# Tree attention on one core: three stores one block of loads back, and three heads instead of two stored apart in pieces of 116 rows

## The chip, the cores and the metric

The kernel runs on one core of a Trainium2 chip. The core has five instruction streams that run beside each other and meet at semaphores: TensorE (PE in the profile, with its weight loads as PEld), VectorE (DVE), ScalarE (ACT), GpSimd (POOL) and SyncE (SP). Data moves between HBM and the on-chip memory SBUF through 16 DMA engines, which POOL, SP and ACT feed with transfers. The metric is the time of one execution on the device in microseconds (us), as the median of several runs. The profile is of one further execution.

## The reference

Q, K and V are float32 arrays of shape 8 x 12 x 512 x 64 (batch, heads, positions, dimension), which makes 96 independent heads. Position i is a node of a binary tree whose parent is (i - 1) // 2. A position attends to itself and to its ancestors only:

```python
scores = np.einsum('bhqd,bhkd->bhqk', Q, K) * scale          # scale = 1 / sqrt(64)
scores = scores + (1 - mask) * (-1e9)                        # mask: itself and its ancestors
weights = np.exp(scores - np.max(scores, axis=-1, keepdims=True))
weights = weights / (np.sum(weights, axis=-1, keepdims=True) + 1e-10)
return np.einsum('bhqk,bhkd->bhqd', weights, V).astype(np.float32)
```

Each of Q, K, V and the output has 12.58 MB, and one head of one array has 128 KB.

## The kernel before

The 96 heads are worked on in 48 pairs. The main loop runs over i, and in its round i it forms the scores of pair i on PE (`scores1`, `scores2`), takes their exponentials on ACT, multiplies the weights of pair i - 1 by V on PE (`values`) and divides by the sums on DVE (`norm`, the line L735, which writes the output tile `of`). Only those parts of the score matrix are formed that the tree can reach. In between, `turn` transposes K and Q of later pairs on PE (into `ktp` and `qtp`), and DVE copies the result to SBUF. DVE, ACT and POOL also lay out V in the form that `values` wants (`spread`, L374).

A head's 512 positions lie in SBUF as 128 partitions of 4 positions each, so that a partition of one head holds 1 KB of float32 output. In what follows a row is such a partition's 1 KB. Output tiles hold 8 heads (1 MB, heads 8b to 8b + 7 for block b), and from pair 16 on four consecutive pairs fill one tile: pair 36 has the heads 72 and 76, pair 37 has 73 and 77, pair 38 has 74 and 78, pair 39 has 75 and 79.

POOL issues nearly all DMAs. Loads of K and Q bring 8 heads at a time late in the kernel (`load_k`, `load_q` with the block's first head, 1 MB read from HBM and 512 KB written to SBUF, since the load turns float32 to bfloat16). Loads of V bring 16 heads in pieces (`load_rows`: `upper` is half of them, `leaves0` and `leaves1` a quarter each). A store of a block is 1 MB. All of POOL's transfers go through one queue (q0 in the profile, called software_dynamic). SP and ACT have queues of their own (q1 and q10, hardware_dynamic); they carry the first loads, the heads that are stored apart, and the last pairs' stores.

The order on POOL is a list, written by `pool_program` (L759). In each round, `pool(i)` (L878) takes operations from its front for as long as `ready` allows them; the operation is put into POOL's program there, and on the chip it then waits for its semaphores alone. Two kinds of waits matter. POOL's DMAs take turns on eight semaphores (DMASW0 to DMASW7), so that each waits until the eighth DMA before it has landed. And a load waits until the readers of its buffer are done (4 buffers each for K and Q, 3 for V, 10 output tiles).

In the list before, the loads of K and Q go from block 56 to block 88 in steps of 8 heads, and behind each pair of loads stands one store, 56 heads behind (`BEHIND`). `lay_beside` (L443) is a POOL copy of a whole K or Q tile into another layout, made for the blocks 80 and 88; the transposes of these blocks (L507, L566) read the copy. Behind the loads the list has the other stores, with the copies between them.

`store_apart` (L753) is called once, behind round 38. It stores the heads 72 and 73 from SP, each as 116 rows and as 12 rows. POOL's store of that block then has six heads instead of eight.

Of the kernel before, what the change touches and what calls it, by code (L numbers as in the profile page):

```python
# [10 lines left out]
CODE = 2048.0  # L11
CODE_ROWS = 40
NOUT = 20
BEHIND = 56

# [104 lines left out]
def kernel(  # L120
# [7 lines left out]
    nc = tc.nc  # L128
    B, H, S, D = Q.shape
    P = nc.NUM_PARTITIONS  # L130
    assert S == 512 and D == 64 and P == 128 and (B * H) % 4 == 0
    scale = float(1.0 / np.sqrt(D))
    NH = B * H
# [3 lines left out]
    KB, VB = 8, 16  # L137
# [459 lines left out]
    def scores1(i):  # L597

        sp = psS.tile([P, 2, 512], fp32, name="s1")
        for a in range(2):  # L600
            nc.tensor.matmul(  # L601
                out=sp[:, a, :],
                lhsT=(k1code if i < WIDE else k1wide)[64 * a:64 * a + CODE_ROWS, :],
                rhs=(q1code, q1wide, q1far)[(i >= WIDE) + (i >= FAR)][64 * a:64 * a + CODE_ROWS],
                start=True, stop=False,
            )
        for a in range(2):
            nc.tensor.matmul(  # L608
                out=sp[:, a, :], lhsT=keys(i, a, TOP),
                rhs=qTs[i][64 * a:64 * a + 64, :, :].rearrange("p t c -> p (t c)"),  # L610
                start=False, stop=True,
            )
        et = etpool.tile([P, 2, 4, 128], bf16, name="e1")
        nc.scalar.activation(  # L614
            out=et[:, :, :, :].rearrange("p a t c -> p (a t c)"),
            in_=sp[:, :, :].rearrange("p a c -> p (a c)"),
            func=AF.Exp, scale=scale,
        ) if i < WIDE else nc.scalar.activation(  # L618
            out=et[:, :, :, :].rearrange("p a t (r u) -> p a (t r) u", u=2 if i < FAR else 4),
            in_=sp[:, :, :].rearrange("p a (u c) -> p a c u", u=2 if i < FAR else 4),  # L620
            func=AF.Exp, scale=scale,
        )
        ets[i] = et
# [102 lines left out]
    def norm(i):  # L726
        j, r = divmod(i, 4)
        if r == 0:
            ofs[j] = opool.tile([P, 8, 4, D], fp32, name="of")
        o4 = obs[i][:, :, 0:260].rearrange("p a (t c) -> p a t c", c=D + 1)  # L730
        rec = small.tile([P, 2, 4, 1], fp32, name="rec")
        for a, n in ((0, 2),) if i < NP - 1 else ((0, 1), (1, 1)):
            nc.vector.reciprocal(out=rec[:, a:a + n, :, :], in_=o4[:, a:a + n, :, D:D + 1])  # L733
            h0, h1 = [head(i, x) % 8 for x in (a, a + n - 1)]
            nc.vector.tensor_tensor(  # L735
                out=ofs[j][:, h0:h1 + 1:head(i, 1) - head(i, 0), :, :],
                in0=o4[:, a:a + n, :, 0:D],
                in1=rec[:, a:a + n, :, :].to_broadcast([P, n, 4, D]),
                op=ALU.mult,
            )  # L740

    def store(eng, h0, n, step=1, p0=0, p1=P):
        return eng.dma_start(  # L743
            out=Or[p0:p1, h0:h0 + step * (n - 1) + 1:step, :],
            in_=ofs[h0 // 8][p0:p1, h0 % 8:h0 % 8 + step * (n - 1) + 1:step, :, :].rearrange(
                "p h t d -> p h (t d)"
            ),
        )


    APART, APART_AT, APART_ROWS = 72, 38, 116

    def store_apart():  # L753

        for p0, p1 in ((0, APART_ROWS), (APART_ROWS, P)):
            for h in range(2):
                store(nc.sync, APART + h, 1, 1, p0, p1)

    def pool_program():  # L759

        ops = [
            (load_k, 2, 2), (load_q, 2, 2), (load_v, 0, 4), (load_v, 4, 4),
            (load_k, 4, 2), (load_k, 6, 2), (load_q, 4, 2), (load_k, 8, 4),
            (load_q, 6, 2), (load_q, 8, 4), (load_v, 8, 8), (load_k, 12, 4),
            (load_q, 12, 4), (load_k, 16, 4), (load_rows, 1, "upper"),
            (load_q, 16, 4), (load_rows, 1, "even"), (load_k, 20, 4), (load_rows, 1, "odd"),
            (load_q, 20, 4), (load_k, 24, 8), (load_q, 24, 4), (load_rows, 2, "upper"),
            (load_q, 28, 4), (load_rows, 2, "leaves0", "leaves1"), (load_k, 32, 8), (load_q, 32, 8),
            (load_rows, 3, "upper"),
            (spread_pool, (1, "Z0", 8, 16), (1, "Z1", 8, 16), (1, 6, 8, 16), (1, 9, 8, 16)),  # L770
            (load_q, 40, 8), (load_k, 40, 8), (load_rows, 3, "leaves0", "leaves1"), (load_k, 48, 8),
            (spread_top, 2), (spread_pool, (2, "Z0", 0, 16), (2, "Z1", 0, 16)), (load_q, 48, 8),
            (spread_pool, (2, "X", 0, 16), (2, "M", 0, 16), (2, "D1", 0, 16)), (spread_top, 3, 0, 12),
            (load_rows, 4, "upper"), (spread_top, 3, 12, 16),
        ]
        loaded, stored = 72, 0
        for h in range(56, NH, KB):
            top = [(spread_top, h // VB + 0)] if h % VB == 8 and 4 <= h // VB + 0 < NH // VB else []
            if top:
                top.append((spread_pool, (h // VB, "Z0", 0, 16), (h // VB, "Z1", 0, 16)))  # L780
            ops += [(load_k, h, KB)] + top + [(load_q, h, KB)]
            if h == 64:
                ops.append((
                    spread_pool, *[(3, part, 0, 16) for part in ("Z0", "Z1", "X", "M", "D1")]
                ))
            while loaded < min(h + 32, NH):
                names = ("leaves0", "leaves1") if loaded % VB else ("upper",)
                ops.append((load_rows, loaded // VB) + names)
                loaded += KB
            if top:  # L790
                o = h // VB
                ops.append((spread_pool, *[(o, part, 0, 16) for part in ("X", "M", "D1")]))
            if stored + KB + BEHIND <= h + KB:
                ops.append((store, nc.gpsimd, stored, KB))
                stored += KB
        ops.insert(-1, (lay_beside, "kst", 80 // KB))
        while stored < NH - KB:
            n = 2 if stored == APART else 0
            ops.append((store, nc.gpsimd, stored + n, KB - n))
            if stored == 40:  # L800
                ops.append((lay_beside, "qst", 80 // KB))
            if stored == 64:
                ops += [(lay_beside, "kst", 88 // KB), (lay_beside, "qst", 88 // KB)]
            stored += KB
        ops += [(store, nc.gpsimd, NH - KB + h, 2) for h in (0, 4)]
        return ops

# [57 lines left out]
    def spread_by(copy, table, steady, i):  # L865
# [7 lines left out]
        for args in todo:  # L873
            spread(copy, *args)

    program = pool_program()

    def pool(i):  # L878
        while program and ready(program[0], i):
            op = program.pop(0)  # L880
            op[0](*op[1:])
# [18 lines left out]
    for i in range(NP + 1):  # L900
        steps = FIRST[i] if i < len(FIRST) else "SVK" if i % 2 else "SVQ"
        if i >= max(FAR, KFAR - 4):
            steps = ("SVK", "SVQ", "SVK", "SQV")[i % 4]
        elif i == FAR - 1:
            steps = "SQVK"
        for step in steps:
            if step == "S" and i < NP:
                scores1(i)
                scores2(i)
            if step == "V" and i >= 1:  # L910
                values(i - 1)
# [12 lines left out]
            if step == "D":  # L924
                spread_by(nc.vector.tensor_copy, BY_VECTOR, STEADY_VECTOR, i)
            if step == "A":
                spread_by(nc.scalar.copy, BY_SCALAR, STEADY_SCALAR, i)
        if "D" not in steps:
            spread_by(nc.vector.tensor_copy, BY_VECTOR, STEADY_VECTOR, i)
        if "A" not in steps:  # L930
            spread_by(nc.scalar.copy, BY_SCALAR, STEADY_SCALAR, i)
        pool(i)
        if i == APART_AT:
            store_apart()
        if i == NP - 1:
            for p in (0, P // 2):
                for a, eng in enumerate((nc.sync, nc.scalar)):
                    store(eng, head(i - 1, a), 1, 1, p, p + P // 2)
# [34 lines left out]
```

## Time and profile before

| | us |
|---|---|
| median of 3 runs (lowest, highest) | 132.93 (132.81, 133.04) |
| the profiled execution, its own time | 132.49 |
| its span, from the first instruction to the last | 130.7 |
| PE busy in it | 113.7 (87%) |
| DVE busy | 105.6 (81%) |
| ACT busy | 101.1 (77%) |
| POOL busy | 84.4 (65%) |
| granted TensorE clock, mean | 0.986 |

The profiled execution is 0.44 us under the median, and 1.8 us of its time lie outside the span. The first load of K lands near 4.5 us, the last work on DVE ends at 127.0 us, and what then follows up to the span's end is the landing of the last stores.

How to read the rows that follow. A row of a timeline gives the start in us from the span's start, the duration, the engine, the line, the operation and its tiles (out<-in), and in brackets the idle time before it and what ended it. For SP and ACT queues the row covers several issues from the first to the last. A row of the windows gives a stretch, its length, the busy time of each engine with its number of instructions, the TensorE clock, the mean busy share of the 16 DMA engines and the rate in GB/s of what was written. Packets of a DMA engine can overlap, so that the share of busy DMA engines can lie above 1. A row of a DMA queue gives the number of packets, the MB written and the time of the packets as a share of 16 engines' time in that stretch. MB are millions of bytes, KB are 1024.

### The profile page before, as it was taken

To read this page: it belongs to the slowest core of one execution; us is meant where nothing else is said; L and a number is where in the kernel's file an instruction comes from. 1 tells how busy PE (TensorE), PEld (TensorE's weight loads), DVE (VectorE), ACT (ScalarE), POOL (GpSimd) and SP (SyncE) were. 2 spreads that over 40 slices of the span, in tenths; PEclk is the share of its full clock that TensorE was granted. 3 is DMA by queue.
4 is the path that set the end of the run, shared out by engine and by line. 5 is a ranking of instruction groups with operands and counts; after the bars stand their busy time and mean duration, and the time that the engine had idled before them with its cause. 6 is when DMAs were issued, how large, how long until landed. Compare 5 with 4: busy or idle time off the path is not lost.

```text
span 130.7 us, 5436 instructions
## 1 busy us (share of the span) xinstructions
PE 113.7 (87%) x2353; PEld 81.0 (62%) x2353; DVE 105.6 (81%) x254; ACT 101.1 (77%) x163; POOL 84.4 (65%) x116
## 2 busy tenths in 40 slices
PE   6688969999799887899998999896999997999940
PEld 2354755766577566677776786674677675776630
DVE  3349779888999998989998998987898997894560
ACT  4179676989779995968987799797689785889930
POOL 6999625354483999995299899953999963202130
PEclk9999999999999999999999999999999999999995
DMA  2999999999999999999999999999999999999984
GB/s 89 248 190 192 201 195 201 201 202 205 201 203 208 208 205 207 208 210 205 207 211 201 283 292 210 270 309 231 338 228 322 257 277 397 402 404 386 382 339 145
DMA packets 26071, 32.25 MB, mean 247 GB/s; under 512 B 1240, under 2 KB 19544, under 8 KB 26048
## 3 DMA queue, kind: packets, MB, share of 16 engines
q0 software_dynamic: 24384, 30.41, 111.4%
q1 hardware_dynamic: 944, 0.91, 2.2%
q10 hardware_dynamic: 720, 0.59, 1.5%
q8 instruction: 18, 0.29, 0.8%
q14 instruction: 5, 0.04, 0.1%
HBM read 37.94 MB, written 12.58 MB: 386 GB/s over the span
## 4 chain that ended last, share of the span: by engine, by line
DVE 29%; DMA 28%; PE 22%; POOL 7%; ACT 6%; issue 4%; ACTq 0%; DVEq 0%; POOLq 0%
DMA vst<-in_V_dram 17%; DMA qst<-in_Q_dram 11%; DVE of L735 9%; PE ob L696 8%; DVE vt L374 6%; PE s L601 3%; DVE qq L577 3%; ACT e L652 3%; DVE rec L733 3%; DVE kk L521 3%; POOL kst L247 2%; PE s L608 2%; DVE kk L525 2%; POOL qst L247 2%; ACT e L618 2%
## 5 line engine op out<-in xcount | busy, mean ns | idle before, releaser
L618 ACT ACTIVATE e<-s 128x1024 bf16<-128x1024 f32 x40 | 40.9, 1024 | 15.0 <-PE s L608 14.6
L696 PE MATMUL ob<-vt,e 128*128 128x65 bf16 (+1 forms) x940 | 37.1, 197 | 2.6 <-DVE of L735 1.0
L696 PEld LDWEIGHTS <-e 128*128 128x128 bf16 (+1 forms) x960 | 30.1, 102 | 9.6 <-DVE of L735 1.9
L374 POOL COPY vt<-vst 32x512 int32<-32x512 int32 (+4 forms) x44 | 32.5, 739 | 4.7 <-PE ob L696 2.5
L652 ACT ACTIVATE e<-s 128x384 bf16<-128x384 f32 x80 | 34.7, 490 | 0.0
L735 DVE TENSOR_TENSOR of<-ob,rec 128x512 f32<-128x512 f32 x47 | 32.5, 691 | 1.6
L374 DVE COPY vt<-vst 32x1024 bf16<-32x1024 bf16 (+5 forms) x47 | 20.9, 445 | 2.8 <-DMA vst<-in_V_dram 1.9
L743 POOL DMA_DIRECT2D out_dram<-of x13 | 11.5, 888 | 12.9 <-DVE of L735 12.4
L733 DVE RECIPROCAL rec<-ob 128x8 f32<-128x8 f32 x47 | 9.5, 202 | 9.9 <-PE ob L696 9.3
L257 POOL DMA_DIRECT2D kst<-in_K_dram x11 | 8.0, 725 | 7.4 <-DMA qst<-in_Q_dram 3.2
L601 PE MATMUL s<-far,codes 40*128 40x512 bf16 x64 | 12.5, 386 | 0.0
L635 PEld LDWEIGHTS <-codes 40*128 40x128 bf16 x80 | 6.2, 94 | 8.7 <-issue 3.9
L614 ACT ACTIVATE e<-s 128x1024 bf16<-128x1024 f32 x8 | 8.2, 1023 | 4.1 <-PE s L608 4.0
L577 DVE COPY qq<-qtp 128x1024 bf16<-128x1024 bf16 x16 | 10.9, 680 | 0.3 <-PE qtp L572 0.3
L635 PE MATMUL s<-far,codes 40*128 40x384 bf16 x64 | 10.7, 324 | 0.4 <-ACT e L652 0.2
L257 POOL DMA_DIRECT2D qst<-in_Q_dram x12 | 8.5, 708 | 3.8 <-DMA vst<-in_V_dram 1.9
L374 ACT COPY vt<-vst 32x512 int32<-32x512 int32 (+3 forms) x19 | 10.4, 545 | 0.4
L608 PE MATMUL s<-qq,kk 64*128 64x512 bf16 x48 | 9.2, 378 | 1.0 <-DVE qq L577 1.0
L646 PEld LDWEIGHTS <-kk 64*128 64x128 bf16 x192 | 8.4, 94 | 2.6
L521 DVE COPY kk<-ktp 128x256 bf16<-128x256 bf16 x24 | 9.0, 414 | 0.7 <-PE ktp L513 0.7
L302 POOL DMA_DIRECT2D vst<-in_V_dram x7 | 5.6, 800 | 6.0 <-DMA vst<-in_V_dram 4.3
L572 PE MATMUL qtp<-ptile,qst 128*64 128x128 bf16 x192 | 7.5, 221 | 1.7 <-DVE qq L577 1.0
(64 smaller groups left out, 178.2 us busy)
## 6 DMA issues: line engine op xcount, KB each, us to landing
out_dram<-of POOLq DMA_DIRECT2D x10, 1024.0 KB, 15.2
kst<-in_K_dram POOLq DMA_DIRECT2D x9, 512.0 KB, 16.5
qst<-in_Q_dram POOLq DMA_DIRECT2D x8, 512.0 KB, 14.8
vst<-in_V_dram POOLq DMA_DIRECT2D x12, 256.0 KB, 13.5
vst<-in_V_dram POOLq DMA_DIRECT2D x6, 512.0 KB, 12.9
qst<-in_Q_dram POOLq DMA_DIRECT2D x6, 256.0 KB, 12.1
kst<-in_K_dram POOLq DMA_DIRECT2D x4, 256.0 KB, 10.3
out_dram<-of POOLq DMA_DIRECT2D x1, 768.0 KB, 13.0
```

The lines of the kernel that those rows point to most:

```text
L257: return nc.gpsimd.dma_start(out=kept[b][:, h0 % KB:h0 % KB + n, :, :].rearrange("p (g x) t d -> p g (x t d)", x=x), in_=src[:, h0 // x:(h ...
L374: return copy(out=dst, in_=src)
L521: nc.vector.tensor_copy(out=columns(flat, 32 * unit, (640, 4), (step, 2), (4, 8), (1, 4)), in_=columns(kp, base, (256, 4), (128, 2), (1, 8 ...
L577: nc.vector.tensor_copy(out=qqs[j][:, :, 8 * last:8 * last + 8, :].rearrange("p b u c -> p b (u c)"), in_=quarters,)
L601: nc.tensor.matmul(out=sp[:, a, :], lhsT=(k1code if i < WIDE else k1wide)[64 * a:64 * a + CODE_ROWS, :], rhs=(q1code, q1wide, q1far)[(i >= ...
L608: nc.tensor.matmul(out=sp[:, a, :], lhsT=keys(i, a, TOP), rhs=qTs[i][64 * a:64 * a + 64, :, :].rearrange("p t c -> p (t c)"), start=False, ...
L618: ) if i < WIDE else nc.scalar.activation(
L635: nc.tensor.matmul(out=flat[:, a, :, :].rearrange("p u (t c) -> p u t c", t=4)[:, :, :, 32 // n:], lhsT=k2wide[64 * a:64 * a + CODE_ROWS, ...
L652: nc.scalar.activation(out=e2s[i % NE][:, a, :, 32:128].rearrange("p t (r u) -> p t r u", u=n), in_=flat[:, a, :, :].rearrange("p u (t r) ...
L696: nc.tensor.matmul(out=ob[lo:hi, a, 65 * t:65 * t + 65], lhsT=e[:, a, PLACE[t], lo:hi], rhs=vt[vtile[tile_v][0]][:, head(i, a) % VB, vtile ...
L733: nc.vector.reciprocal(out=rec[:, a:a + n, :, :], in_=o4[:, a:a + n, :, D:D + 1])
L735: nc.vector.tensor_tensor(out=ofs[j][:, h0:h1 + 1:head(i, 1) - head(i, 0), :, :], in0=o4[:, a:a + n, :, 0:D], in1=rec[:, a:a + n, :, :].to ...
```

## The change

The general loop that wrote the late part of the list is replaced by the list itself. In it, the stores of blocks 8, 16 and 24 stand one block of K and Q loads later than before. The load of V's last `upper` part (heads 80 to 95) moves from ahead of the first store to behind its `leaves`. The two copies of block 80 stand together ahead of the six stores 24 to 64, where before the Q copy stood behind two of five stores. `store_apart` now takes three heads: the 116 rows of heads 72 and 73 behind round 38, and behind round 39 the 116 rows of head 74 and then the 12 rows of all three heads as one DMA. POOL's store of that block has five heads.

```diff
-BEHIND = 56
...
-    APART, APART_AT, APART_ROWS = 72, 38, 116
-
-    def store_apart():
-
-        for p0, p1 in ((0, APART_ROWS), (APART_ROWS, P)):
-            for h in range(2):
-                store(nc.sync, APART + h, 1, 1, p0, p1)
+    APART, APARTS, APART_AT, APART_ROWS = 72, 3, 38, 116
+
+    def store_apart(i):
+
+        if i == APART_AT:
+            for h in range(APARTS - 1):
+                store(nc.sync, APART + h, 1, 1, 0, APART_ROWS)
+        if i == APART_AT + 1:
+            store(nc.sync, APART + APARTS - 1, 1, 1, 0, APART_ROWS)
+            store(nc.sync, APART, APARTS, 1, APART_ROWS, P)
...
-        loaded, stored = 72, 0
-        for h in range(56, NH, KB):
...
-            ops += [(load_k, h, KB)] + top + [(load_q, h, KB)]
...
-            if stored + KB + BEHIND <= h + KB:
-                ops.append((store, nc.gpsimd, stored, KB))
-                stored += KB
-        ops.insert(-1, (lay_beside, "kst", 80 // KB))
-        while stored < NH - KB:
-            n = 2 if stored == APART else 0
-            ops.append((store, nc.gpsimd, stored + n, KB - n))
-            if stored == 40:
-                ops.append((lay_beside, "qst", 80 // KB))
-            if stored == 64:
-                ops += [(lay_beside, "kst", 88 // KB), (lay_beside, "qst", 88 // KB)]
-            stored += KB
...
+        ops += k7 + q7 + leaves(4) + out(0)
+        ops += k8 + q8 + [(spread_pool, *[(3, part, 0, 16) for part in ("Z0", "Z1", "X", "M", "D1")])]
+        ops += leaves(5) + [(load_rows, 5, "upper")]
+        ops += k9 + tops(4) + q9 + rest(4) + out(8)
+        ops += k10 + q10 + out(16)
+        ops += k11 + tops(5) + q11 + rest(5)
+        ops += [(lay_beside, "kst", 80 // KB), (lay_beside, "qst", 80 // KB)]
+        for h in range(24, 72, KB):
+            ops += out(h)
+        ops += [(lay_beside, "kst", 88 // KB), (lay_beside, "qst", 88 // KB)]
+        for h in range(72, NH - KB, KB):
+            n = APARTS if h == APART else 0
+            ops += out(h + n, KB - n)
         ops += [(store, nc.gpsimd, NH - KB + h, 2) for h in (0, 4)]
         return ops
...
-        if i == APART_AT:
-            store_apart()
+        store_apart(i)
```

In the new list `k7` and `q7` are the loads of block 56, `k8` to `k11` those of blocks 64 to 88; `tops(o)` and `rest(o)` are the copies of V by POOL for the 16 heads from 16o, and `out(h)` is the store of the block from head h.

What the change moves on the engines stands in the programs' rows. On POOL, between the load of Q's block 72 and the load of K's block 88 (`of_597`, `of_875` and `of_1151` are the output tiles of blocks 8, 16 and 24), the program before reads:

```order
L257 DMA qst_1937<-in_Q_dram 128x2x1024 [waits DMASW0_49]
L374 COPY vt0_2_117<-vst_1390 32x32x32 x2
L374 COPY vt0_1_116<-vst_1390 32x8x2x32
L743 DMA out_0_dram<-of_875 128x8x256 [waits DMASW1_49]
L257 DMA kst_2007<-in_K_dram 128x2x1024 [waits DMASW2_49]
L257 DMA qst_2009<-in_Q_dram 128x2x1024 [waits DMASW3_49]
L743 DMA out_0_dram<-of_1151 128x8x256 [waits DMASW4_49]
L257 DMA kst_2268<-in_K_dram 128x2x1024 [waits DMASW5_49,PE_49]
```

The same place of the program after the change:

```order
L256 DMA qst_1936<-in_Q_dram 128x2x1024 [waits DMASW7_49]
L373 COPY vt0_2_117<-vst_1390 32x32x32 x2
L373 COPY vt0_1_116<-vst_1390 32x8x2x32
L742 DMA out_0_dram<-of_597 128x8x256 [waits DMASW0_49]
L256 DMA kst_2006<-in_K_dram 128x2x1024 [waits DMASW1_49]
L256 DMA qst_2008<-in_Q_dram 128x2x1024 [waits DMASW2_49]
L742 DMA out_0_dram<-of_875 128x8x256 [waits DMASW3_49]
L256 DMA kst_2267<-in_K_dram 128x2x1024 [waits DMASW4_49,PE_49]
```

At each place of a store now stands the store of the block before it, so that one store fewer lies ahead of these loads in the queue.

On POOL behind the loads, from the copy of K's block 80 to the copies of block 88 (`kst<-kst` and `qst<-qst` are the copies by `lay_beside`; the stores are of blocks 32 to 64), the program before reads:

```order
L448 COPY kst_2536<-kst_2007 128x1024 [waits DMASW2_49,Pool_49]
L743 DMA out_0_dram<-of_1443 128x8x256 [waits DMASW7_49,DVE_49]
L743 DMA out_0_dram<-of_1701 128x8x256 [waits DMASW0_49,DVE_49]
L448 COPY qst_2540<-qst_2009 128x1024 [waits DMASW3_49]
L743 DMA out_0_dram<-of_1984 128x8x256 [waits DMASW1_49,DVE_49]
L743 DMA out_0_dram<-of_2244 128x8x256 [waits DVE_49]
L743 DMA out_0_dram<-of_2512 128x8x256 [waits DVE_49]
L448 COPY kst_2784<-kst_2268 128x1024 [waits DMASW5_49,PE_49]
L448 COPY qst_2786<-qst_2466 128x1024 [waits DMASW6_49,PE_49]
L743 DMA out_0_dram<-of_2769 128x6x256 [waits DMASW4_49,DVE_49]
```

After the change it reads, with the store of block 24 (`of_1151`) as the first of six:

```order
L447 COPY kst_2535<-kst_2006 128x1024 [waits DMASW1_49,Pool_49]
L447 COPY qst_2537<-qst_2008 128x1024 [waits DMASW2_49]
L742 DMA out_0_dram<-of_1151 128x8x256 [waits DMASW6_49]
L742 DMA out_0_dram<-of_1444 128x8x256 [waits DMASW7_49,DVE_49]
L742 DMA out_0_dram<-of_1711 128x8x256 [waits DMASW0_49,DVE_49]
L742 DMA out_0_dram<-of_1983 128x8x256 [waits DVE_49]
L742 DMA out_0_dram<-of_2243 128x8x256 [waits DVE_49]
L742 DMA out_0_dram<-of_2511 128x8x256 [waits DMASW3_49,DVE_49]
L447 COPY kst_2784<-kst_2267 128x1024 [waits DMASW4_49,PE_49]
L447 COPY qst_2786<-qst_2465 128x1024 [waits DMASW5_49,PE_49]
L742 DMA out_0_dram<-of_2769 128x5x256 [waits DVE_49]
```

The copy of Q's block 80 moved ahead of all these stores, and the last store there has five heads instead of six.

On SP, the whole of its stores (`of_2769` is the tile of block 72, `of_3206` the last one; DMAHW0 to DMAHW7 are eight semaphores that the DMAs of SP and ACT share in turn) reads before:

```order
L743 DMA out_0_dram<-of_2769 116x256 [waits DVE_49] x2
L743 DMA out_0_dram<-of_2769 12x256
L743 DMA out_0_dram<-of_2769 12x256 [waits DMAHW0_49]
L743 DMA out_0_dram<-of_3206 64x256 [waits DMAHW2_49,DVE_49]
L743 DMA out_0_dram<-of_3206 64x256 [waits DMAHW4_49]
L743 DMA out_0_dram<-of_3206 64x256 [waits DMAHW5_49,DVE_49]
L743 DMA out_0_dram<-of_3206 64x256 [waits DMAHW7_49]
```

After the change:

```order
L742 DMA out_0_dram<-of_2769 116x256 [waits DVE_49] x3
L742 DMA out_0_dram<-of_2769 12x3x256 [waits DMAHW0_49]
L742 DMA out_0_dram<-of_3206 64x256 [waits DMAHW2_49,DVE_49]
L742 DMA out_0_dram<-of_3206 64x256 [waits DMAHW4_49]
L742 DMA out_0_dram<-of_3206 64x256 [waits DMAHW5_49,DVE_49]
L742 DMA out_0_dram<-of_3206 64x256 [waits DMAHW7_49]
```

SP has four stores apart as before. The third of them, which was a store of 12 rows, is now one of 116, and the semaphore DMAHW7 that the very last store waits for is then the one of that third store. The instructions of PE, DVE and ACT and their order are the same in both programs.

More of the change, by code (lines that the diff above doesn't have):

```diff
@@ L775, in pool_program @@
         ]
-        loaded, stored = 72, 0
-        for h in range(56, NH, KB):
-            top = [(spread_top, h // VB + 0)] if h % VB == 8 and 4 <= h // VB + 0 < NH // VB else []
-            if top:
-                top.append((spread_pool, (h // VB, "Z0", 0, 16), (h // VB, "Z1", 0, 16)))
-            ops += [(load_k, h, KB)] + top + [(load_q, h, KB)]
[L782 to L792, printed above, removed]
-            if stored + KB + BEHIND <= h + KB:
-                ops.append((store, nc.gpsimd, stored, KB))
-                stored += KB
@@ L796, in pool_program, with tops @@
-        ops.insert(-1, (lay_beside, "kst", 80 // KB))
-        while stored < NH - KB:
-            n = 2 if stored == APART else 0
-            ops.append((store, nc.gpsimd, stored + n, KB - n))
-            if stored == 40:
-                ops.append((lay_beside, "qst", 80 // KB))
-            if stored == 64:
-                ops += [(lay_beside, "kst", 88 // KB), (lay_beside, "qst", 88 // KB)]
-            stored += KB
+        def tops(o):
+            return [(spread_top, o), (spread_pool, (o, "Z0", 0, 16), (o, "Z1", 0, 16))]
@@ new lines, in rest, with out, leaves, qk @@
+        def rest(o):
+            return [(spread_pool, (o, "X", 0, 16), (o, "M", 0, 16), (o, "D1", 0, 16))]
+        def out(h0, n=KB):
+            return [(store, nc.gpsimd, h0, n)]
+        def leaves(o):
+            return [(load_rows, o, "leaves0", "leaves1")]
+        def qk(h0):
+            return [(load_k, h0, KB)], [(load_q, h0, KB)]
+        k7, q7 = qk(56)
+        k8, q8 = qk(64)
+        k9, q9 = qk(72)
+        k10, q10 = qk(80)
+        k11, q11 = qk(88)
+        ops += k7 + q7 + leaves(4) + out(0)
```

## The prediction

> **What bounds the kernel now.** I read the span in slices first, for the state of the DMA engines, and then the windows, to see where that state ends. From the page, the row of the 40 slices and the HBM line:
>
> ```profile
> DMA  2999999999999999999999999999999999999984
> HBM read 37.94 MB, written 12.58 MB: 386 GB/s over the span
> ```
>
> The DMA engines are over nine tenths busy in every slice but the first and the last two. The windows put numbers to it (the last two columns are the DMA share and the GB/s written):
>
> ```profile
> core 0: us, PE busy (x) PEld busy (x) DVE busy (x) ACT busy (x) POOL busy (x), PEclk, DMA share, GB/s
> 5.00:108.00 103.00, 93.48 (x2022) 67.76 (x2022) 90.73 (x212) 85.33 (x137) 76.28 (x103) 1.00 1.24 228
> 108.00:120.00 12.00, 11.07 (x213) 8.17 (x213) 9.43 (x22) 9.31 (x16) 1.87 (x2) 1.00 1.03 401
> 120.00:129.00 9.00, 5.56 (x118) 3.86 (x112) 3.82 (x10) 4.99 (x9) 2.31 (x3) 0.90 0.92 343
> 129.00:130.70 1.70, 0.00 (x0) 0.00 (x0) 0.00 (x0) 0.00 (x0) 0.00 (x0) 0.50 0.12 39
> ```
>
> Up to 108 us loads and stores are mixed, from there only stores are left. Full engines show 1.03 there, and between 120 and 129 us it is still 0.92. The total of bytes doesn't change with their order, so the stores alone could end the kernel earlier by no more than the idle share, (1.03 - 0.92) x 9 us = 1.0 us, and only if the load were even over the engines.
>
> Then the chain of waits, in the part where it leaves the computing engines, and at its end:
>
> ```profile
> 76.94 0.23 PE s L608 x2
> ...
> 77.19 1.03 POOL vt L374
> ...
> 78.26 0.99 POOL vt L374
> 79.25 14.58 DMA qst<-in_Q_dram
> ...
> 93.87 0.64 PE qtp L572 x16
> ```
>
> ```profile
> 126.55 0.42 DVE of L735
> ```
>
> From 93.87 us on the chain runs through PE, DVE and ACT without a DMA, and it ends at 126.97 us; 3.7 us of stores follow. So there are two bounds side by side: computing, which waits for a few loads and then runs 33.1 us, and the DMA engines, which are full to about 129 us. The change touches both, with opposite signs.
>
> **Part 1: the loads come earlier.** What PE loses to late loads is in its timeline, where only waits on the late K and Q blocks end an idle time on a DMA:
>
> ```profile
> 80.91 0.64 PE L513 MATMUL ktp<-ptile,kst 128*64 128x128 bf16 x16 [0.23 <-DMA kst<-in_K_dram]
> 83.62 0.64 PE L572 MATMUL qtp<-ptile,qst 128*64 128x128 bf16 x16 [0.45 <-DMA qst<-in_Q_dram]
> 91.38 0.64 PE L513 MATMUL ktp<-ptile,kst 128*64 128x128 bf16 x16 [0.98 <-DMA kst<-in_K_dram]
> 93.87 0.64 PE L572 MATMUL qtp<-ptile,qst 128*64 128x128 bf16 x16 [0.23 <-DMA qst<-in_Q_dram]
> ```
>
> These are blocks 64 and 72, and the waits sum to 0.23 + 0.45 + 0.98 + 0.23 = 1.9 us. After the change one MB less lies ahead of each of them: V's `upper` 5 for block 64, the store of block 8 for block 72. At the 401 GB/s of the second window a store of 1 MB takes 1,048,576 / 401 = 2.6 us, and a load reads as much. 2.6 us earlier is more than the longest wait, even with PE itself ahead by the 1.9 us, so I take all four away: the last work on DVE ends at about 126.97 - 1.9 = 125.1 us. POOL does not hold them back: Q's block 72 is issued at 79.25 us, 14.6 us ahead of its landing, and behind the same copies as after the change. `upper` 5 lands behind both `leaves`, near 86.5 us at 2.6 us a MB, and its first reader on POOL started at 90.23 us (next rows), or 88.3 with all 1.9 us gained: nothing waits.
>
> POOL's late rows carry the price of the copies' new places:
>
> ```profile
> 90.23 4.87 POOL L374 COPY vt<-vst 32x512 int32<-32x512 int32 x6 [2.49 <-PE ob L696]
> ...
> 98.93 1.04 POOL L448 COPY kst<-kst 128x1024 int32<-128x1024 int32 x1 [0.19 <-DMA kst<-in_K_dram]
> 99.92 1.79 POOL L743 DMA_DIRECT2D out_dram<-of  x2
> 101.70 1.05 POOL L448 COPY qst<-qst 128x1024 int32<-128x1024 int32 x1
> 102.68 2.86 POOL L743 DMA_DIRECT2D out_dram<-of  x3
> 106.43 1.04 POOL L448 COPY kst<-kst 128x1024 int32<-128x1024 int32 x1 [0.89 <-DMA kst<-in_K_dram]
> 108.91 1.04 POOL L448 COPY qst<-qst 128x1024 int32<-128x1024 int32 x1 [1.43 <-DMA qst<-in_Q_dram]
> ```
>
> A store costs POOL (1.79 + 2.86) / 5 = 0.93 us, six cost 5.6. Even if POOL came no earlier to 98.9 us, two copies of 1.04 and six stores bring it to 106.6 us, where K's block 88 was copied at 106.43; that block then has landed 2.6 us earlier, and Q's follows at once, at 107.6 instead of 108.91. Q's block 80 is copied at about 100 us instead of 101.70. The copies' readers come no sooner than 1.9 us earlier, so these moves cost nothing. The queue doesn't run dry either: block 24's store now is issued near 101 us, and what is ahead of it (store 16, K and Q of 88) lasts to about 106.
>
> Price on the path: 1.9 us gained by computing, and nothing by itself at the end, for as long as the DMA engines are full to 129 us.
>
> **Part 2: the third head apart.** The rows of the queues between 115 and 119 us, where from SP only the 116 rows of head 73 are under way:
>
> ```profile
> q0 software_dynamic: 394, 1.50, 95.3%
> q1 hardware_dynamic: 86, 0.09, 6.2%
> ```
>
> A packet of q1 (one row of 1 KB) takes 0.062 x 16 x 4 us / 86 = 46 ns; one of q0 takes 0.953 x 16 x 4 / 394 = 155 ns, and q0 moves 1.50 MB in 61.0 us of engine time, 24.6 bytes a ns, so 8 KB in 0.33 us. An engine that takes turns between both queues gets a row through every 46 + 155 = 201 ns, or 5.0 a us. What passes is 86 / 4 = 21.5 a us. That is what four engines do, not sixteen: each of them carries 29 of the 116 rows.
>
> The Trainium skill, page "DMA: Bandwidth & Descriptors", section "Issuing engines are not separate DMA queues", says that DMAs started by different engines end up on the same 16 DMA engines, so that a second issuer saves only the time of issuing. By it the third head would cost the engines nothing and save them nothing, and the sum would be zero for this part. The 21.5 rows a us speak against reading it as an even load.
>
> So the third head adds 29 rows and, if the 12 rows go to as many engines, one of these, on the four engines: 30 x 46 ns = 1.38 us, and takes the head's eighth share of POOL's store off every engine, 8 rows or 8 KB, 0.33 us. Net: +1.05 us on four engines, -0.33 on the others, or -0.28 with one of the 12 rows. Whether this ends the kernel later depends on which engines are last. A row of the end says something about it, 127.4 to 127.8 us:
>
> ```profile
> q1 hardware_dynamic: 56, 0.05, 39.4%
> q10 hardware_dynamic: 42, 0.03, 28.2%
> q0 software_dynamic: 8, 0.03, 18.2%
> ```
>
> POOL's queue then is busy for 0.182 x 16 = 2.9 engines: three or four engines still have POOL's stores when the others are through with them. That is the number of those that carried the two heads, which put them 2 x (1.05 + 0.3) = 2.7 us behind where they would be beside the rest. The bounds are -0.33 us (they are not the last ones at all, and the others end the kernel) and +1.05 (they are, and nothing is behind them). The last row is nearer to the upper end; since the latest of the four need not be quite the last engine, I take three quarters of it, +0.8 us.
>
> The issue of it costs nothing: SP has no other work, and POOL issues one store as before. A wait is added, though. SP's rows and ACT's at the end:
>
> ```profile
> 104.30 23.84 SPq L743 DMA_DIRECT2D out_dram<-of  x8
> ```
>
> ```profile
> 125.67 2.46 SPq L743 DMA_DIRECT2D out_dram<-of  x4
> 125.67 2.09 ACTq L743 DMA_DIRECT2D out_dram<-of  x3
> ```
>
> The last of SP's four stores there now waits for the landing of head 74's 116 rows. 29 rows at 201 ns take 5.8 us a head. In 108 to 112 us q1 already moves 104 packets:
>
> ```profile
> q0 software_dynamic: 384, 1.47, 93.4%
> q1 hardware_dynamic: 104, 0.10, 7.0%
> ```
>
> Three heads from 108 us are through at 108 + 17.5 = 125.5, and with computing earlier they start earlier. The store that waits was issued by 128.1 (104.30 + 23.84), so there is cover of about 2 us, or none if the last store comes 1.9 us earlier, and then it lands no later than before.
>
> **The sum.** Span 130.7 + 0.8 = 131.5 us; the profiled execution's own time 132.49 + 0.8 = 133.3. It lies 0.44 us under the median of the runs, so the median becomes 132.93 + 0.8 = 133.7 us.
>
> **The rivals.**
>
> *Faster: the four engines have room.* If at the end the last engines are others, the ones with 116 rows must be at least 1.05 + 0.33 = 1.4 us ahead of them for the full gain, and 1.05 for none. Then all others end 0.33 us earlier, and the computing that ends 1.9 us earlier fills up to 1.0 us of idle share. That gives -0.3 to -1.0, in the middle 132.3 us. The 2.9 engines of the last row speak against it, as their number fits; that the row doesn't name engines speaks for it. The same page of the Trainium skill, section "Latency and other measured facts", says that the engines 7 and 15 usually are slower than the rest; were these the last here, this rival would hold. No view of this trace names an engine.
>
> *No change.* The latest of the four is some 0.8 to 1.3 us ahead of the last engine, and the two shifts cancel: 132.9 us, a chance of 0.11. The same time comes out if the rows are spread evenly over the engines after all, as the first rule of the page would have it; with the 21.5 rows a us I give that 0.03.
>
> *Slower by more.* Head 74's rows come late: they queue behind heads 72 and 73 on four engines, and SP's last store waits for them. It decides if they land behind 128.1 us. Two heads begun at 108 end near 119.6, so it takes a start of the third behind 122 us. The price is what the store is late plus its own landing, about +0.8 more, 134.5 us.
>
> **How the numbers follow.** A measurement of this kernel tells about 0.2%, 0.27 us, from no change. Forecast +0.8 us: chance 0.56. Slower by more: 0.08. No change within 0.2%: 0.14. Faster: 0.22. So slower 0.64, same 0.14, faster 0.22. The forecast's own range is +0.4 to +1.1 us, 133.3 to 134.0. The range that is to hold the time reaches down into the faster case to 132.4 and up to 134.2.
>
> **What would show it.** Right: the four waits on DMA gone from PE, the last DVE work near 125.1 us, Q's block 72 landing near 91.3, q1 passing still about 21 packets a us but for 17 us instead of 12, and the DMA windows full to about 130 us on a small share of engines: a lower share between 120 and 129 us with a longer tail. Wrong: a tail that ends earlier with the share above 0.92, or DVE's last work no earlier than 126.5 us, which would mean that another wait took the place of those on the loads.

## The result, and the profile after

| | before | after |
|---|---|---|
| median of 6 runs (lowest, highest), us | 132.87 (132.60, 133.04) | 133.51 (133.35, 133.62) |
| after / before, 95% interval | | 1.0049 [1.0034, 1.0064] |
| the profiled execution, its own time | 132.49 | 133.44 |
| its span | 130.7 | 131.6 |

The kernel became slower by half a per cent, 0.64 us, although its computing ended earlier. The page of after first, the row of the 40 slices, then its windows in the stretches that were shown of before:

```profile
DMA  3999999999999999999999999999999999999981
```

```profile
core 0: us, PE busy (x) PEld busy (x) DVE busy (x) ACT busy (x) POOL busy (x), PEclk, DMA share, GB/s
...
108.00:120.00 12.00, 11.76 (x228) 8.47 (x226) 8.92 (x20) 10.29 (x19) 1.81 (x2) 1.00 1.03 400
120.00:129.00 9.00, 3.51 (x74) 2.48 (x74) 2.92 (x8) 3.11 (x6) 1.46 (x2) 0.83 0.90 337
129.00:131.60 2.60, 0.00 (x0) 0.00 (x0) 0.00 (x0) 0.00 (x0) 0.00 (x0) 0.50 0.07 23
```

PE, DVE and ACT have clearly less left to do behind 120 us (PE 3.51 us instead of 5.56), while the DMA share there falls from 0.92 to 0.90. The tail behind 129 us is longer, 2.6 us instead of 1.7, and thinner: the last slice of the page is busy to one tenth instead of four. Where computing gained, the PE timeline shows: the transposes of the blocks 64 and 72 have no wait on a DMA ahead of them any more.

```profile
79.49 0.61 PE L512 MATMUL ktp<-ptile,kst 128*64 128x128 bf16 x16
81.60 0.61 PE L571 MATMUL qtp<-ptile,qst 128*64 128x128 bf16 x16
...
89.07 0.61 PE L512 MATMUL ktp<-ptile,kst 128*64 128x128 bf16 x16
91.14 0.61 PE L571 MATMUL qtp<-ptile,qst 128*64 128x128 bf16 x16
```

POOL's timeline has the load of Q's block 72 and the copies with the stores at their new places; the row of its queue behind it is that load's, with its median time from issue to landing in the last column:

```profile
77.68 0.71 POOL L256 DMA_DIRECT2D qst<-in_Q_dram  x1
...
89.06 4.88 POOL L373 COPY vt<-vst 32x512 int32<-32x512 int32 x6 [3.88 <-PE ob L695]
...
99.67 5.42 POOL L742 DMA_DIRECT2D out_dram<-of  x6
105.09 1.05 POOL L447 COPY kst<-kst 128x1024 int32<-128x1024 int32 x1
106.07 1.05 POOL L447 COPY qst<-qst 128x1024 int32<-128x1024 int32 x1
```

```profile
qst<-in_Q_dram POOLq DMA_DIRECT2D x1, 512.0 KB, 13.2
```

It lands at 77.68 + 13.2 = 90.9 us. The reader of V's `upper` waits for PE and not for a DMA, and the copies of block 88 come earlier than before. The chain of waits again leaves the computing engines behind DVE's last work, now at 124.51 + 0.42 = 124.93 us, 2.04 us earlier:

```profile
124.51 0.42 DVE of L734
```

But 6.7 us of stores follow it up to the span's end, where it was 3.7. The queues' rows between 115 and 119 us, and those of SP's queue in the stretches 119 to 122 and 122 to 125 us:

```profile
q0 software_dynamic: 394, 1.50, 95.7%
q1 hardware_dynamic: 85, 0.08, 5.9%
...
q1 hardware_dynamic: 63, 0.06, 6.0%
...
q1 hardware_dynamic: 57, 0.05, 4.8%
```

SP's rows pass at the rate of before, 85 / 4 = 21 a us, but for longer: before, 119 to 122 us had 26 packets and 122 to 125 us none. And POOL's queue, which before had 8 packets between 127.4 and 127.8 us and none behind 128.2, now in steps of 0.4 us from 127.4 on:

```profile
q0 software_dynamic: 16, 0.05, 29.0%
...
q0 software_dynamic: 6, 0.02, 10.5%
...
q0 software_dynamic: 5, 0.02, 10.2%
...
q0 software_dynamic: 4, 0.01, 7.8%
```

0.102 x 16 = 1.6 and then 0.078 x 16 = 1.2 engines' worth of POOL's stores is still under way, up to 129 us, some 0.8 us longer than before.

### The profile page after: what moved, and what is told of

Read it like the earlier page. It is cut to its first block, busy times and chain, and to the rows that moved or that the text cites. A ratio compares the mean times of both kernels' runs of the same rounds, so it can differ in the third digit from the quotient of the medians.

```text
span 131.6 us, 5436 instructions
## 1 busy us (share of the span) xinstructions
PE 114.4 (87%) x2353; PEld 81.3 (62%) x2353; DVE 107.5 (82%) x254; ACT 101.1 (77%) x163; POOL 84.7 (64%) x116
## 4 chain that ended last, share of the span: by engine, by line
DVE 40%; PE 23%; DMA 19%; POOL 6%; ACT 4%; issue 3%; ACTq 0%; POOLq 0%
DVE of L734 13%; DMA qst<-in_Q_dram 11%; PE ob L695 8%; DVE vt L373 8%; DMA vst<-in_V_dram 7%; DVE qq L576 5%; DVE kk L520 5%; DVE kk L524 4%; DVE rec L732 4%; PE s L600 3%; POOL kst L246 2%; PE s L607 2%; POOL qst L246 2%; ACT e L651 2%; PE qtp L571 2%
## 5 line engine op out<-in xcount | busy, mean ns | idle before, releaser
L617 ACT ACTIVATE e<-s 128x1024 bf16<-128x1024 f32 x40 | 40.9, 1024 | 13.2 <-PE s L607 12.7
L373 DVE COPY vt<-vst 32x1024 bf16<-32x1024 bf16 (+5 forms) x47 | 22.8, 486 | 2.2 <-DMA vst<-in_V_dram 1.3
L645 PE MATMUL s<-qq,kk 64*128 64x160 bf16 (+1 forms) x192 | 8.9, 208 | 0.0
```

The lines of the kernel that those rows point to most:

```text
L373: return copy(out=dst, in_=src)
L645: nc.tensor.matmul(out=flat[:, a, :, lo:hi], lhsT=keys(i, a, WTILE2[t]), rhs=qT[64 * a:64 * a + 64, :, lo:hi], start=False, stop=t == 1, s ...
```

## The experiments

All ratios are to runs of the kernel before on the same chip, and the intervals are of 95%.

**The new order with two heads apart** (against after):

```diff
-    APART, APARTS, APART_AT, APART_ROWS = 72, 3, 38, 116
+    APART, APARTS, APART_AT, APART_ROWS = 72, 2, 38, 116
...
-            for h in range(APARTS - 1):
+            for h in range(APARTS):
                 store(nc.sync, APART + h, 1, 1, 0, APART_ROWS)
-        if i == APART_AT + 1:
-            store(nc.sync, APART + APARTS - 1, 1, 1, 0, APART_ROWS)
-            store(nc.sync, APART, APARTS, 1, APART_ROWS, P)
+            for h in range(APARTS):
+                store(nc.sync, APART + h, 1, 1, APART_ROWS, P)
```

> The new order of the list, but two heads apart as before. Theory (the DMA engines are full to the end, and four of them carry the 116 rows): the third head's net 1.05 us on the four engines is gone, and the order moves no bytes between engines, so the time is that of the kernel before within 0.3 us, 132.6 to 133.0, although the last work on DVE ends near 125 us as in the changed kernel. Rival A (the new order itself costs the time): it stays near 133.5. Rival B (earlier loads are worth what PE waited): 131.0 to 132.0.

**The old order with three heads apart** (against before):

```diff
...
+        if i == APART_AT:
+            for h in range(APARTS - 1):
+                store(nc.sync, APART + h, 1, 1, 0, APART_ROWS)
+        if i == APART_AT + 1:
+            store(nc.sync, APART + APARTS - 1, 1, 1, 0, APART_ROWS)
+            store(nc.sync, APART, APARTS, 1, APART_ROWS, P)
...
-            n = 2 if stored == APART else 0
+            n = APARTS if stored == APART else 0
...
-        if i == APART_AT:
-            store_apart()
+        store_apart(i)
```

> The old order of the list with three heads apart in 116 rows. Theory: the third head alone brings the loss, 133.4 to 133.8, with POOL's queue ending later on a few engines, and the last work on DVE near 127 us as before. Rival A (the order costs): 132.7 to 133.0.

**The new order with no head apart** (against after):

```diff
-            n = APARTS if h == APART else 0
+            n = 0
...
-        store_apart(i)
```

> The new order with no head apart; POOL stores all of block 72. Theory (what counts is the fullest engine): the four engines lose 2 x 1.05 us against two heads and are the first to be through, and all others get 2 x 0.3 us more, so the end is 0.4 to 0.7 us later than with two heads, 133.2 to 133.6. Rival C (each head apart costs something, so fewer are better): at most the time with two heads, 132.9 or less.

**The new order with one head apart**: as with two, with `APARTS` at 1.

> The new order with one head apart, in 116 and 12 rows. Theory (the fullest engine decides, and the best number is where the four engines and the others are through together): between none (134.06) and two (133.06), as the others still get 0.3 us more than with two heads, 133.3 to 133.7. Rival C (each head apart costs): at most 133.06.

| order | heads apart | median, us | ratio to before |
|---|---|---|---|
| new | 0 | 134.06 | 1.0077 [1.0052, 1.0101] |
| new | 1 | 133.48 | 1.0037 [1.0012, 1.0062] |
| new | 2 | 133.06 | 1.0017 [0.9994, 1.0039] |
| new | 3 (after) | 133.51 | 1.0049 [1.0034, 1.0064] |
| old | 2 (before) | | 1 |
| old | 3 | 133.45 | 1.0030 [1.0002, 1.0058] |

The row with one head is from another chip than the rows with none and with two; the median of before was 133.1 us there, so the ratios are what can be compared. Three heads in the old order and one head in the new one came out within what was expected. Two heads in the new order are 0.06 us above their range, and none apart, 134.06, is 0.46 us above its own.

The new order alone makes no difference that can be told, and the third head alone makes most of the loss: 0.0030 x 132.9 = 0.40 us in the old order (by the interval 0.03 to 0.77), (1.0049 - 1.0017) x 132.9 = 0.43 us in the new one. It isn't so that every head apart costs something: from none to two the kernel becomes faster, by (1.0077 - 1.0017) x 132.9 = 0.80 us, with one head between them (its 0.27 us from two can't be told from nothing), and only the third makes it slower. With none apart the time is the longest, and POOL's queue has packets at the end too; its rows from 127.8 us on, in steps of 0.4 us:

```profile
q0 software_dynamic: 8, 0.02, 15.8%
...
q0 software_dynamic: 8, 0.02, 15.7%
...
q0 software_dynamic: 3, 0.01, 7.7%
```

At 128.2 to 128.6 us that is 0.157 x 16 = 2.5 engines' worth, and the 8 packets can be on eight of the sixteen engines at most. So some engines are late even when no head is stored apart. The ends of the spans go with this. In the traces of before, of the new order with two heads, of after and of none apart, the last of these steps with more than 1% from POOL's queue end at 128.2, 128.6, 129.0 and 129.8 us, and the spans end 2.5, 2.5, 2.6 and 2.9 us behind them. A reading that fits is a balance: the heads apart take bytes off the late engines and put rows on four others, until with the third head the four are the last. That is argued and not shown, since no view names an engine.

Where the new order's gain went, these rows tell: the last work on DVE, with the span in the answer's first line, for the new order with two heads, with none, and the old order with three.

```profile
core 0 of [0], span 131.1 us
...
125.60 0.42 DVE L734 TENSOR_TENSOR of<-s,rec 128x256 f32<-128x256 f32 x1
```

```profile
core 0 of [0], span 132.7 us
...
125.47 0.42 DVE L734 TENSOR_TENSOR of<-s,rec 128x256 f32<-128x256 f32 x1
```

```profile
core 0 of [0], span 131.5 us
...
126.23 0.42 DVE L735 TENSOR_TENSOR of<-s,rec 128x256 f32<-128x256 f32 x1
```

With two heads, computing ends at 126.02 us, 0.95 earlier than before, and the span is no shorter: 5.1 us of stores follow instead of 3.7. What computing gains, the DMA engines don't pass on.

**One store of 1 MB less, in the kernel before and in the one after**. This asks how far below the DMA engines the computing bound lies. Against before:

```diff
-            ops.append((store, nc.gpsimd, stored + n, KB - n))
+            if stored != 56:
+                ops.append((store, nc.gpsimd, stored + n, KB - n))
```

> The kernel before without POOL's store of block 56 (heads 56 to 63 of the output are left out), 2.6 us less for each DMA engine behind the last load. Theory: the DMA engines would be through near 127.2 us, so computing, which ends at 127.0 and is followed by its stores, becomes the bound: 132.4 to 132.8, only 0.1 to 0.5 faster than with the store.

Against after:

```diff
-        for h in range(24, 72, KB):
+        for h in (24, 32, 40, 48, 64):
             ops += out(h)
```

> The changed kernel without POOL's store of block 56 (heads 56 to 63 of the output are left out). Theory: here computing ends near 125 us, so that the 2.6 us that the engines have less show nearly in full: 130.9 to 131.6, 1.2 us or more faster than the kernel before without the same store. So the earlier loads are worth 1 to 2 us as soon as the engines aren't full to the end. Rival E (the four engines or SP's last store, which waits for the third head's rows, hold it back whatever POOL's queue has): 132.5 or more.

Measured: before without the store 132.18 us, 0.9930 [0.9898, 0.9962]; after without it 131.41 us, 0.9858 [0.9817, 0.9900]. The windows, DVE's last work and the spans, first of before without the store:

```profile
120.00:125.00 5.00, 4.81 (x104) 3.36 (x98) 2.18 (x6) 4.80 (x9) 2.00 (x3) 1.00 0.65 249
125.00:129.00 4.00, 0.62 (x14) 0.41 (x12) 1.63 (x5) 0.05 (x1) 0.30 (x1) 0.74 0.80 264
```

```profile
core 0 of [0], span 130.5 us
...
126.42 0.42 DVE L735 TENSOR_TENSOR of<-s,rec 128x256 f32<-128x256 f32 x1
```

and of after without it:

```profile
120.00:125.00 5.00, 4.56 (x88) 3.02 (x84) 2.86 (x7) 3.99 (x8) 1.62 (x3) 1.00 0.80 309
125.00:129.00 4.00, 0.00 (x0) 0.00 (x0) 0.94 (x3) 0.00 (x0) 0.00 (x0) 0.58 0.66 206
```

```profile
core 0 of [0], span 129.7 us
...
125.56 0.42 DVE L734 TENSOR_TENSOR of<-s,rec 128x256 f32<-128x256 f32 x1
```

Both now have idle DMA engines behind 120 us (0.65 and 0.80), and both end 3.7 us behind DVE's last work (126.84 and 125.98 us). That is the time of the last pairs' stores when nothing is ahead of them: here computing is the bound. Before is 0.7% above that, 0.7 us by the medians and 0.9 by the ratio, against the 2.6 us that the store takes: its two bounds lie about 1 us apart or less (by the interval 0.5 to 1.4). The theory had put it at 132.4 or more; it was 0.2 us lower. After falls from 1.0049 to 0.9858, which is 2.5 us and nearly the whole store. And the difference between the two, 132.18 - 131.41 = 0.77 us by the medians and (0.9930 - 0.9858) x 132.84 = 0.96 by the ratios, is what the earlier loads are worth to a kernel that is not bound by its stores. The two intervals leave about 0.7 us either way, so the 1.2 us or more that were expected were not reached, but are not excluded.

**Three heads apart in other pieces.** `APART_ROWS` is all that changes against after:

```diff
-    APART, APARTS, APART_AT, APART_ROWS = 72, 3, 38, 116
+    APART, APARTS, APART_AT, APART_ROWS = 72, 3, 38, 119
```

and likewise 115 and 112.

> The changed kernel with the three heads cut at 119 rows instead of 116. If the rows of such a store go to as many engines as divide them (7 x 17, where 4 x 29 make 116), then a head adds 18 rows of 46 ns, 0.83 us, and takes off 0.33, so +0.5 us on seven engines. Theory: three heads are +1.5 us on each of the seven, where two in 116 rows were +2.1 on four, and the others get 0.3 us less than before: if the three further engines have room, 132.4 to 132.8, else up to 133.4; in any case less than the changed kernel. Rival C (the number of heads apart is what costs): 133.5 as the changed kernel.

> The changed kernel with the three heads cut at 115 rows, 5 x 23. Theory (the fullest engines decide): a head adds 24 rows of 46 ns, 1.1 us, less 0.33, so three heads put +2.3 us on five engines, where two in 116 rows put +2.1 on four and three +3.15. The end comes 0.6 to 0.9 us earlier than in the changed kernel if the fifth engine has the room that the four have, 132.6 to 133.0, and near 133.3 if it has none, as two of the seven had in the run with 119 rows. Rival C (the number of heads apart costs): 133.5.

> The changed kernel with the three heads cut at 112 rows, 16 x 7, and the other 16 rows one to an engine. Theory: every engine then carries the same share whether SP or POOL issues it, so no engine is relieved and none is loaded, and the time is that of the kernel with no head apart, 133.7 to 134.2, slower than the changed kernel, although SP's rows go through at a higher rate than 21 a us. Rival D (SP's stores are too slow on four engines, and that is the loss): faster than the changed kernel, 133.0 or less.

Measured: 119 rows 133.31 us, 1.0037 [1.0021, 1.0052]; 115 rows 133.52 us, 1.0047 [1.0029, 1.0066]; 112 rows 133.80 us, 1.0056 [1.0031, 1.0081]. SP's queue between 108 and 112 us, where the first heads' rows are under way, with 116 rows (after), 115, 119 and 112:

```profile
q1 hardware_dynamic: 84, 0.09, 6.0%
```

```profile
q1 hardware_dynamic: 101, 0.10, 7.4%
```

```profile
q1 hardware_dynamic: 146, 0.14, 10.2%
```

```profile
q1 hardware_dynamic: 227, 0.21, 15.2%
```

That is 21, 25, 36.5 and 57 rows a us. If the rows of a store go to the largest number of engines up to 16 that divides them, 116 = 4 x 29, 115 = 5 x 23, 119 = 7 x 17 and 112 = 16 x 7, then it is 5.3, 5.1, 5.2 and 3.5 rows a us for each engine. The first three are near the 5.0 that the prediction worked out for an engine that takes turns between both queues; why the sixteen get less no run shows. The Trainium skill, page "DMA: Bandwidth & Descriptors", section "Why a DMA increments its semaphore by 16 and not by 1", says that a DMA from SP or ACT is split over the largest number up to 16 that divides the size of its slowest dimension on both sides, and runs on the lowest-numbered engines. For the number of engines the trace agrees, with the 5.1 to 5.3 rows an engine; which engines they are no view shows.

The time doesn't follow the number of engines. With four, five, seven and sixteen the ratios are 1.0049, 1.0047, 1.0037 and 1.0056, and none can be told from after's. So the loss is not that SP's rows pass slowly: with 57 rows a us the kernel is no faster than with 21. With 119 rows the time lies at the upper end of what the theory of the balance allowed (133.4), with 112 rows inside its range, and with 115 rows 0.2 us above it, at the 133.5 of rival C. So rival C, that three heads apart cost what they cost in whatever pieces, stands beside the balance. For the balance to hold, the engines that get rows only with 115 or 119 would have to end about as late as the four, which no view can show.

**Two heads in pieces of 116 rows and two in pieces of 120** (against after):

```diff
-    APART, APARTS, APART_AT, APART_ROWS = 72, 3, 38, 116
+    APART, APARTS, APART_AT, APART_ROWS = 72, 4, 38, 116
...
-            for h in range(APARTS - 1):
+            for h in range(2):
                 store(nc.sync, APART + h, 1, 1, 0, APART_ROWS)
-        if i == APART_AT + 1:
-            store(nc.sync, APART + APARTS - 1, 1, 1, 0, APART_ROWS)
-            store(nc.sync, APART, APARTS, 1, APART_ROWS, P)
+            store(nc.sync, APART, 2, 1, APART_ROWS, P)
+        if i == APART_AT + 2:
+            store(nc.sync, APART + 2, 2, 1, 0, 120)
+            store(nc.sync, APART + 2, 2, 1, 120, P)
```

> The new order with the heads 72 and 73 in 116 and 12 rows and the heads 74 and 75 in 120 and 8 rows, so that POOL stores four heads of the block. 120 rows are 15 x 8: fifteen engines carry what they would carry from POOL, one is relieved of 0.33 us a head. If the one engine that lags alone at the end is that one (the Trainium skill, page "DMA: Bandwidth & Descriptors", section "Latency and other measured facts", calls 7 and 15 usually slower), the time falls to 132.5 to 132.9; if it is another, it stays at that of two heads in the new order, 132.9 to 133.2. Rival C (the number of heads apart costs): 133.5 or more.

Measured: 133.38 us, 1.0026 [1.0002, 1.0050], between what was expected of another late engine (up to 133.2) and of rival C (133.5 or more). That is no better than two heads apart alone (1.0017, well inside this interval), so a single late engine that these 120 rows would pass by is not what ends the kernel, or the rows put as much on others as they take from it; the run doesn't tell these apart. Four heads apart at 1.0026, less than three at 1.0049, speak against a cost that grows with each head, but the interval reaches up to the three. No version that writes the whole output was faster than the kernel before.

## Why the prediction was right, and where it was not

**Two bounds side by side.** Right. Without one store, before ends 3.7 us behind DVE's last work, as it does with all its stores, and is faster by 0.7 to 0.9 us, where the store takes the engines 2.6: computing lay that close under the DMA engines.

**Part 1, the loads.** The four waits went, Q's block 72 landed at 90.9 us (91.3 foretold), the last DVE work ended at 124.93 (125.1), and the POOL copies' moves cost nothing. Waits of PE on these loads are in all three traces of the old order and in none of the nine of the new one. But that the end of this one execution fits the 1.9 us is partly chance. The division of pair 24 on DVE lies ahead of all four waits; its rows, of before, of after and of the new order with two heads, and then of before and of after without block 56's store:

```profile
74.37 0.69 DVE L735 TENSOR_TENSOR of<-ob,rec 128x512 f32<-128x512 f32 x1
```

```profile
73.33 0.69 DVE L734 TENSOR_TENSOR of<-ob,rec 128x512 f32<-128x512 f32 x1
```

```profile
74.61 0.69 DVE L734 TENSOR_TENSOR of<-ob,rec 128x512 f32<-128x512 f32 x1
```

```profile
73.93 0.69 DVE L735 TENSOR_TENSOR of<-ob,rec 128x512 f32<-128x512 f32 x1
```

```profile
74.64 0.69 DVE L734 TENSOR_TENSOR of<-ob,rec 128x512 f32<-128x512 f32 x1
```

After was ahead by 75.06 - 74.02 = 1.0 us already there. From there to the last DVE work before takes 126.97 - 75.06 = 51.9 us, after 50.9 and the new order with two heads 126.02 - 75.30 = 50.7; without the store it is 126.84 - 74.62 = 52.2 us before and 125.98 - 75.33 = 50.65 after. All three traces of the old order have 51.9 to 52.9 us, all nine of the new one 50.6 to 51.0. So the earlier loads are worth 0.9 to 2.3 us by the traces, 1.55 between the means, and 0.8 to 1.0 by the times of the two runs without block 56, with some 0.7 us either way. The 1.9 us lie in the upper part of this; that the gain is less is likely and not shown. At the end the gain was worth nothing, since the DMA engines were full, as the prediction had it. The new order with two heads shows it, with computing 0.95 us earlier and a time of 1.0017 [0.9994, 1.0039].

**Part 2, the third head.** The size was off, and the mechanism is shown only in part. What held: the rows pass at 21 a us as four engines would do it, and faster where more engines divide them; POOL's queue lasts longer on a few engines; and the third head by itself makes the kernel slower in both orders. What is not shown is the step between, that the four engines with the rows are the ones that end last. The sign that the prediction took for it, 2.9 engines' worth of POOL's queue at 127.4 us, is none: with no head apart 2.5 engines' worth is left even at 128.2 us. And with the rows in pieces for five, seven or sixteen engines the time can't be told from that with four. So why the third head costs time stays open; the balance between engines is the reading that also gives a reason for the gain of the first two heads.

The size was 0.40 and 0.43 us instead of 0.8. If the balance is the reason, the term that was mis-sized is the "three quarters" of the upper bound. It supposed that the four engines were nearly the last ones already with two heads; with 1.05 us more on them and 0.4 us at the end, they were some 0.6 us ahead of the last engine, an estimate by that model alone.

**The sum.** 131.5 us of span, 133.3 of the profiled execution and 133.7 of the median were foretold; 131.6, 133.44 and 133.51 came. The median's error is -0.2 us: the third head at 0.4 instead of 0.8, and 0.0017 x 132.9 = 0.2 us from the new order, which was put at nothing and whose interval includes zero. That the two errors partly cancel is luck.

**The rivals.** Faster: that the third head takes time off falls with its price in both orders. No change: by the same estimate its place, 0.8 to 1.3 us of room, was missed by little, and the even spread falls with the 57 rows a us that 112 rows show beside 21. Slower by more did not occur. SP's row of after:

```profile
102.71 24.34 SPq L742 DMA_DIRECT2D out_dram<-of  x8
```

SP's last store was issued by 127.05 us, 2.1 us behind DVE's last work instead of 1.2 before; but the run with three heads of 119 rows, which has the same wait, reads:

```profile
core 0 of [0], span 131.6 us
...
103.00 23.34 SPq L742 DMA_DIRECT2D out_dram<-of  x8
```

```profile
124.78 0.42 DVE L734 TENSOR_TENSOR of<-s,rec 128x256 f32<-128x256 f32 x1
```

There the last issue, at 126.34 us, is 1.1 us behind DVE's 125.20, and the span is 131.6 us as well. After without block 56's store has its last issue at 127.14 us, as late as after, and its span is only 129.7 us:

```profile
103.77 23.37 SPq L742 DMA_DIRECT2D out_dram<-of  x8
```

So the late issue is not what ends the kernel.

## What to carry to other kernels

Where computing and transfers end within a microsecond of each other, removing waits from one buys nothing until the other is relieved; take one transfer out, see by how much the time falls, and the distance of the two bounds is known, to within the noise, before any order is tuned. How many heads to store apart only a series of runs told: two were 0.80 us better than none, and the third took about half of that back. What the removal of a wait is worth is read from the stretch behind it and from several executions; the end of one execution also holds what happened ahead of the wait, here 1.0 us.

## What was not expected of the hardware

SP's rows start late where loads still run. After issued its first 116 rows at 102.71 us; the queues' rows between 104 and 106 us, where POOL's queue still brings loads, and between 106 and 108 us read:

```profile
q0 software_dynamic: 216, 0.72, 104.7%
```

```profile
q0 software_dynamic: 203, 0.78, 98.0%
q1 hardware_dynamic: 26, 0.03, 3.7%
```

None of SP's packets is seen for at least 106 - 102.71 = 3.3 us behind the issue. The Trainium skill, page "DMA: Bandwidth & Descriptors", section "Latency and other measured facts", gives about 0.6 us to the first byte of a transfer from such a queue; the trace shows that this doesn't hold at this place. A full queue of POOL alone is not the reason: with no head apart SP issues its first store at 124.60 us, and 10 of its packets are seen between 125.5 and 126 us, at most 1.4 us later, with POOL's queue at 89% there. Whether it is the loads stays open.

The sixteen DMA engines don't end together even with no head apart: 2.5 engines' worth of POOL's queue, 8 packets, was left at 128.2 us, and the kernel was 0.6% slower than with two heads apart. Why these engines are late stays open.
